# First projection whole in front of the recurrence, its input copied to DRAM in eight transfers a half; plain order in place of a permuted one in the block inverse

## The chip, the core and the metric

One NeuronCore of one Trainium2 chip runs the whole program. The metric is device time in microseconds (us), from runs of the whole program; the profile is of one more execution. Engines are named as the profile names them: PE (TensorE matmuls), PEld (its weight loads), DVE (VectorE), ACT (ScalarE), POOL (GpSimd) and SP, whose queue issues all DMA transfers.

## What is computed

A decoder trunk with one RWKV-7 layer and one differential attention layer, 1024 tokens of width 1024, all in float32. The part that the change touches is the first layer:

```
xm   = xn + (x_prev - xn) * mu[p]                      # a mix for each of p = r, k, v, g
r, k, v, g = xm[p] @ w_in[p]                           # four projections, 1024 x 1024 each
w, a = two small two-step projections of mixed inputs  # decay and rate
for t in tokens:                                       # 16 heads, state 64 x 64
    sa    = state @ a_t
    state = state * w_t + sa b_t^T + v_t k_t^T
    y_t   = state @ r_t
x = x + (groupnorm(y) + bonus) * silu(g) @ w_out
```

The second layer (shared keys and values, attention in 8 heads, output projection, final norm) follows and is not touched.

## The kernel before

**Front.** `start` loads x in eight tiles, scales and transposes it into `xnT` in SBUF. `lora` makes the two small projections (`d_c`, `d_a` in DRAM). `projections(hf, src, order, prs)` makes the large ones: for a half of the tokens `hf`, for each `p` in `order` and each block `pr` of 128 output columns, one *step* of 24 matmuls of 128x512 (three for each of 8 blocks of the contraction, since every operand is split into a high and a low part; L197, L198, L199). The first step of each group of one `p` also makes the mixed input `xm` and its two parts: two instructions on ACT (L149, L153) and two on DVE (L144, L156) for each of the 8 blocks. The string `ORD` sets how these three generators are interleaved (`s`, `l`, `f`), and where `xnT` is copied to DRAM (`0`, `1`: one transfer of 2052 KB for each half, L772), from where later steps load their input (`xk`, L756). Before the change the front holds p = 0, 2, 1 of the first half of the tokens for the column blocks 0 to 3 (`lower`).

**Recurrence.** The tokens are cut in chunks of 64. One unit of work (`Ms[n]`, 16 of them) is two chunks for 8 of the 16 heads. Each goes through `prep` (decay products `ar`, `bk`; the matrices within a chunk `pm`; the strictly triangular 32x32 blocks `ab`, by DRAM `dA` into `al` with all 128 blocks side by side), `invert` (31 steps of a triangular solve, each two instructions on POOL, L559 and L561; the result goes by DRAM `dX` into `qd`), `merge` (from 32x32 to 64x64), `chain` (the state passes through both chunks) and `norm`. `slot` emits one slot for each unit: chain of unit i, merge of i+1, invert of i+2, prep of i+3, and between them *fill* from one list: the remaining projection steps (before: the upper column blocks of the first half, then all of the second half, then the gate p = 3) and the first output projection, as much as `FILL` says for the slot. In `chain`, `out` accumulates y from two matmuls for each of 4 head pairs x 2 heads: one against the state (`sv`, 64x64, L637) and one against the solved part (`uv`, 128x64, L640).

**Permutation.** In `prep` the rows of `ar` are written permuted within blocks of 32 (`mixed`, two instructions, L476), `ab` is added through a permuted view (L518) and the mask is built for that order, so that `invert` writes a partition of `xx` to `dX` as one run of 1 KB.

**What sets the order.** A list scheduler places the instructions of each engine and the DMA issues of SP, by its own durations and by the priorities in `PRI`; each engine then runs its list in order. So an edit of `ORD` or `FILL` also changes rows far from it. All transfers are issued by SP, in one list.

Of the kernel before, what the change touches and what calls it, by code (L numbers as in the profile page):

```python
# [20 lines left out]
P = 128  # L21
# [12 lines left out]
XB = 8  # L34
ORD = "sslflsfls01llllflflflflflflflflflflfl"
FILL = [26000] * 8 + [12500] * 12
PRI = {"chain": 2000, "merge": 1500, "invert": 1000, "prep": 500}
# [27 lines left out]
def rsqrt(nc, pool, x, shape, name, steps=3, tiles=None):  # L65
# [8 lines left out]
    return y  # L74


def mixed(x):

    return x.rearrange("p c (k q) -> p c q k", q=4)


class Trunk:
# [144 lines left out]

    def projections(self, hf, src, order, prs=range(KT)):
        for p in order:
            group = {}  # L230
            for pr in prs:
                yield self.proj_step(hf, p, pr, src, group)
# [167 lines left out]
    def wkv_open(self):  # L400
# [18 lines left out]
        for r0 in (0, 64):  # L419
            v = self.pmask[r0:r0 + 64].rearrange("p a (z t) -> p a z t", z=2)  # L420
            for z, order in enumerate(([[32, 2], [1, 4], [4, 8]], [[1, 64]])):
                nc.gpsimd.affine_select(out=v[:, 0, z, :], in_=v[:, 0, z, :], compare_op=ALU.is_ge, fill=0.0,
                                        base=z - 1, channel_multiplier=-1, pattern=order)
        self.bones = cst.tile([P, P], F32, name="bones")
# [23 lines left out]
    def prep(self, M, following):  # L448
# [6 lines left out]
        def ch(x):  # L455
            return x.rearrange("p u (c t) -> p (u c) t", t=C)
# [17 lines left out]
        M["ar"] = ar = ua.tile([P, 8, 2, C], F32, name="ar")  # L474
        for b in range(0, C, 32):
            nc.vector.tensor_tensor(ar[:, :, 0, b:b + 32].rearrange("p c (q k) -> p c q k", q=4), mixed(ch(kraw)[:, :, b:b + 32]),  # L476
                                    mixed(ep[:, :, b:b + 32]), op=ALU.mult)
        nc.vector.tensor_tensor(ar[:, :, 1, :], ch(r), ep[:, :, 1:CW], op=ALU.mult)
# [36 lines left out]
        for b in range(4):  # L515
            bs = slice(32 * b, 32 * b + 32)
            av = ab[bs].rearrange("p c (k q) -> p c k q", q=4)
            nc.vector.tensor_tensor(av, av, pm[bs, b // 2, :, b % 2 * 32:b % 2 * 32 + 32].rearrange("p c (q k) -> p c k q", q=4), op=ALU.add)  # L518
        nc.sync.dma_start(out=dA.rearrange("c x s t -> (x s) c t"), in_=ab)
# [20 lines left out]
    def invert(self, M):  # L540
# [14 lines left out]
        for s in range(31):  # L555
# [6 lines left out]
            yield 0  # L562
        dX = self.dr.tile([32, 4, 8, 32], F32, name="dX")
        nc.sync.dma_start(out=dX.rearrange("x q k t -> q x (k t)"), in_=xx)
        M["qd"] = qd = self.ub.tile([P, 8, 32], F32, name="qd", bufs=1)
        nc.sync.dma_start(out=qd, in_=dX.rearrange("(c x) q k t -> (x q k) c t", c=8))

# [50 lines left out]
    def chain(self, M):  # L618
# [9 lines left out]
        def out(c):  # L628
            if c == 0:
                M["y"] = ps.tile([P, 8, C], F32, name="y", bufs=1)  # L630
            y = M["y"]
            for u in range(NU):
                uc = u * NC + c

                z = M["qt"] + c == 0
                for h in range(0 if z else 2):
                    nc.tensor.matmul(y[HS[h], uc, :], lhsT=sv[HS[h], h, uc, :], rhs=ar[HS[h], uc, 1, :], start=True, stop=False,  # L637
                                     tile_position=(h * 64, h * 64))
                for h in range(2):
                    nc.tensor.matmul(y[HS[h], uc, :], lhsT=uv[:, h, uc, :], rhs=pm[:, h, uc, 64:P], start=z, stop=True,  # L640
                                     tile_position=(0, h * 64))
        for c in range(NC):
# [95 lines left out]
    def layer1(self):  # L738
# [14 lines left out]
        def src_of(hf):  # L753
# [4 lines left out]
            return src  # L758
        lower, upper = range(KT // 2), range(KT // 2, KT)
        with ExitStack() as s1:  # L760
            xnp = s1.enter_context(tc.tile_pool(name="xnp", bufs=1, reuse_waits="tile"))
            lp = s1.enter_context(tc.tile_pool(name="lp", bufs=2, reuse_waits="tile"))
            self.fps = s1.enter_context(tc.tile_pool(name="fps0", bufs=8, space=PSUM, reuse_waits="tile"))
            xnT = xnp.tile([P, KT, S + 1], F32, name="xnT")
            start = self.start(lp, xnT)
            lo = self.lora(lp, xnT)
            first = self.run(self.projections(0, lambda k: xnT[:, k, 0:TH + 1], (0, 2, 1), lower))
            plan = {"s": start, "l": lo, "f": first}
            for c in ORD:
                if c in "01":  # L770
                    hf = int(c)
                    nc.sync.dma_start(out=d_xn[hf].rearrange("k p t -> p k t"), in_=xnT[:, :, hf * TH:hf * TH + TH + 1])  # L772
                    continue
                for _ in range(KT if c == "f" else 1):
                    next(plan[c], None)
            for g in plan.values():
                assert next(g, None) is None
# [3 lines left out]
        def steps():  # L781
            yield from self.projections(0, src_of(0), (0, 2, 1), upper)
            yield from self.projections(1, src_of(1), (0, 2, 1))
# [564 lines left out]
```

## Time and profile before

| | us |
|---|---|
| median of 3 runs | 1670.84 (1669.64 to 1671.71) |
| the profiled execution's own time | 1675.29 |
| its span, first to last instruction | 1673.6 |
| PE, DVE, ACT, POOL busy | 1538.7, 1251.5, 938.2, 691.1 |
| granted TensorE clock, mean over the span | 0.942 |

The span is the time that the views below divide up; the profiled execution has 1.7 us around it, and is 4.5 us above the median. A busy share is an average over stages with different limits; the stages are the front, a stretch in which the first preps and inverts run but no chain yet, the recurrence with its chain, and the second layer. A granted clock of 1.0 is 2.4 GHz and 0.5 is 1.2 GHz; a mean between them is a mix of the two.

### The profile page before, as it was taken

Reading aid. Unit: us, or ns where it says so; the run is one execution under the profiler, and the core shown is the slowest. Engines: PE = TensorE matmul, PEld = TensorE weight load, DVE = VectorE, ACT = ScalarE, POOL = GpSimd, SP = SyncE. Lnnn points to the kernel's source line nnn. Section 1 sums busy time; section 2 is a strip of 40 time slices with the busy share of each in tenths; the row PEclk is TensorE's granted clock in tenths of the full one; section 3 lists DMA queues with packets and bytes.
Section 4 is the critical chain, followed back from the end, with each engine's and each line's share of the span. In section 5 each row is a group of like instructions: output and inputs, shape, how many; then the busy total and the mean of one; then the engine's idle time right before and its main releaser. Section 6 shows DMA issues by size and latency. Waiting matters only on the chain.

```text
span 1673.6 us, 31316 instructions
## 1 busy us (share of the span) xinstructions
PE 1538.7 (92%) x10496; PEld 1227.3 (73%) x10496; DVE 1251.5 (75%) x3183; ACT 938.2 (56%) x2145; POOL 691.1 (41%) x1685
## 2 busy tenths in 40 slices
PE   4699978899899999999899988999999999999897
PEld 3477656677677766677698877788888888888786
DVE  7657888668785686887866767878878788777763
ACT  5556855647555566566543545665656656566421
POOL 4010116778766473787776011233332333323100
PEclk7899978999989978999899899999999999999999
DMA  7655875655565545566556652211111111103331
GB/s 190 177 190 170 247 188 165 191 146 179 167 195 159 145 134 142 171 185 188 146 166 190 178 161 89 76 45 33 45 38 32 45 33 45 39 32 114 98 123 51
DMA packets 207216, 213.70 MB, mean 128 GB/s; under 512 B 62032, under 2 KB 149328, under 8 KB 207056
## 3 DMA queue, kind: packets, MB, share of 16 engines
q1 hardware_dynamic: 207056, 211.71, 43.5%
q8 instruction: 83, 1.36, 0.3%
q14 instruction: 77, 0.63, 0.1%
HBM read 153.39 MB, written 58.27 MB: 126 GB/s over the span
## 4 chain that ended last, share of the span: by engine, by line
PE 59%; DVE 13%; DMA 11%; ACT 7%; issue 5%; POOL 4%; SPq 1%; ACTq 0%; DVEq 0%; POOLq 0%
PE pj L887 6%; PE pj L888 6%; PE pj L889 6%; PE tr L992 4%; PE fl L198 3%; PE fl L197 3%; PE fl L199 3%; PE sc L950 2%; PE sc L951 2%; PE tr L980 2%; POOL xx L561 2%; PE sc L505 2%; DMA wf<-in_a_w_in 2%; POOL tm L559 2%; PE fl L290 1%
## 5 line engine op out<-in xcount | busy, mean ns | idle before, releaser
L197 PE MATMUL fl<-xh,wh 128*128 128x512 f32 x512 | 217.3, 434 | 16.4 <-ACT xh L153 9.3
L559 POOL TENSOR_TENSOR tm<-al,xx 128x60 f32<-128x60 f32 (+24 forms) x496 | 198.7, 401 | 63.7 <-DVE xx L553 27.4
L198 PE MATMUL fl<-xl,wh 128*128 128x512 f32 x512 | 218.4, 428 | 6.2 <-DVE xl L156 6.1
L561 POOL TENSOR_TENSOR xx<-xx,tm 128x60 f32<-128x60 f32 (+24 forms) x496 | 201.9, 407 | 37.4 <-DVE xx L553 1.2
L887 PE MATMUL pj<-wh,xh 128*128 128x512 f32 x512 | 213.3, 417 | 1.6 <-ACT xh L1225 1.6
L199 PE MATMUL fl<-xh,wl 128*128 128x512 f32 x512 | 212.9, 417 | 0.1
L888 PE MATMUL pj<-wh,xl 128*128 128x512 f32 x512 | 202.3, 395 | 2.1 <-DVE xl L1226 2.1
L889 PE MATMUL pj<-wl,xh 128*128 128x512 f32 x512 | 202.0, 394 | 0.0
L956 ACT ACTIVATE p<-sc,mx 128x256 f32<-128x256 f32 (+7 forms) x128 | 94.7, 742 | 140.8 <-DVE mx L955 122.1
L162 DVE TENSOR_TENSOR wl<-wf,wh 128x512 fp32r<-128x512 f32 x160 | 116.8, 734 | 68.6 <-ACT wh L161 61.0
L936 POOL CAST kh<-kh 64x128 fp32r<-64x128 f32 x128 | 44.5, 347 | 260.8 <-ACT kh L928 256.8
L161 ACT CAST wh<-wf 128x512 fp32r<-128x512 f32 x160 | 97.8, 617 | 81.6 <-PE fl L198 51.2
L197 PEld LDWEIGHTS fl<-xh,wh 128*128 128x128 f32 x512 | 101.2, 199 | 47.8 <-ACT xh L153 11.9
L198 PEld LDWEIGHTS fl<-xl,wh 128*128 128x128 f32 x512 | 101.7, 199 | 37.3 <-DVE xl L156 10.0
L199 PEld LDWEIGHTS fl<-xh,wl 128*128 128x128 f32 x512 | 102.1, 199 | 25.1 <-issue 1.9
L889 PEld LDWEIGHTS pj<-wl,xh 128*128 128x128 f32 x512 | 96.5, 188 | 21.6
L888 PEld LDWEIGHTS pj<-wh,xl 128*128 128x128 f32 x512 | 97.0, 189 | 18.6 <-DVE xl L1226 3.3
L887 PEld LDWEIGHTS pj<-wh,xh 128*128 128x128 f32 x512 | 96.9, 189 | 17.5 <-ACT xh L1225 2.5
L954 DVE TENSOR_REDUCE mx<-sc 128x1 f32<-128x256 f32 (+7 forms) x128 | 95.6, 755 | 0.8
L992 PEld LDWEIGHTS tr<-v,p 128*128 128x128 f32 x576 | 74.9, 194 | 7.1 <-ACT p L982 2.4
L505 PE MATMUL sc<-ar,bk 64*128 64x128 f32 x512 | 64.5, 312 | 13.8 <-DVE v L532 3.7
L992 PE MATMUL tr<-v,p 128*128 128x128 f32 x576 | 76.0, 278 | 1.2 <-ACT p L982 1.2
(295 smaller groups left out, 3855.4 us busy)
## 6 DMA issues: line engine op xcount, KB each, us to landing
wf<-in_a_w_in SPq DMA_DIRECT2D x64, 512.0 KB
xk<-d_xn SPq DMA_DIRECT2D x64, 256.5 KB
d_in<-ev SPq DMA_DIRECT2D x64, 256.0 KB
wf<-in_b_w SPq DMA_DIRECT2D x64, 256.0 KB
al<-dA SPq DMA_DIRECT2D x16, 512.0 KB
wf<-in_a_w_out SPq DMA_DIRECT2D x16, 512.0 KB
p<-d_x SPq DMA_DIRECT2D x10, 512.0 KB
d_c<-cc SPq DMA_DIRECT2D x16, 260.0 KB
```

The costliest lines, as they stand in the source:

```text
L161: self.nc.scalar.copy(out=wh, in_=wf)
L162: self.nc.vector.tensor_tensor(wl, wf, wh.bitcast(F32), op=ALU.subtract)
L197: nc.tensor.matmul(G["ps"], lhsT=wh[:, kk, :], rhs=xh, start=(k == 0), stop=False)
L198: nc.tensor.matmul(G["ps"], lhsT=wh[:, kk, :], rhs=xl, start=False, stop=False)
L199: nc.tensor.matmul(G["ps"], lhsT=wl[:, kk, :], rhs=xh, start=False, stop=(k == KT - 1))
L505: nc.tensor.matmul(pp[h][:, i, :], lhsT=bkh(h, c), rhs=ar[h * 64:h * 64 + 64, c].rearrange("p z t -> p (z t)"), start=True, stop=True)
L559: nc.gpsimd.tensor_tensor(tv, al[:, s:s + 1, s + 1:].to_broadcast([P, n, w]), xx[:, 0:n, s:s + 1].to_broadcast([P, n, w]), op=ALU.mult)
L561: nc.gpsimd.tensor_tensor(xx[:, 0:n, s + 1:], xx[:, 0:n, s + 1:], tv, op=ALU.add)
L887: nc.tensor.matmul(pf, lhsT=self.X[i][0][:, k], rhs=wh, start=(k == 0), stop=False)
L888: nc.tensor.matmul(pf, lhsT=self.X[i][1][:, k], rhs=wh, start=False, stop=False)
L889: nc.tensor.matmul(pf, lhsT=self.X[i][0][:, k], rhs=wl, start=False, stop=(k == KT - 1))
L992: nc.tensor.matmul(po, lhsT=at[:, b, :], rhs=H["v"][:, b, :], start=(b == 0), stop=(b == i))
```

## The change

1. `ORD` and `projections`: the front now makes p = 0, 2, 1 of the first half for all 8 column blocks (24 steps in place of 12). The fill list loses these 12 steps and the second making of their three mixed inputs, with 24 loads of `xk`. `FILL` falls from 26000 to 19000 in the first eight slots.
2. The copies of `xnT` to DRAM are made block by block, eight transfers for each half in place of one.
3. The permutation goes: one instruction for `ar` in place of two, a plain add for `ab`, a plain mask; `dX` is laid out so that `invert` writes it in runs of 32 numbers (128 bytes).
4. `out` makes all state matmuls of a chunk first and then all `uv` matmuls, with one start flag for each head row.

```diff
-ORD = "sslflsfls01llllflflflflflflflflflflfl"
-FILL = [26000] * 8 + [12500] * 12
+ORD = "sslflsflsllll" + 10 * "flf1" + 12 * "f00"
+FILL = [19000] * 8 + [12500] * 12
...
-def mixed(x):
-    return x.rearrange("p c (k q) -> p c q k", q=4)
...
-    def projections(self, hf, src, order, prs=range(KT)):
+    def projections(self, hf, src, order):
         for p in order:
             group = {}
-            for pr in prs:
+            for pr in range(KT):
                 yield self.proj_step(hf, p, pr, src, group)
...
-        for b in range(0, C, 32):
-            nc.vector.tensor_tensor(ar[:, :, 0, b:b + 32].rearrange("p c (q k) -> p c q k", q=4), mixed(ch(kraw)[:, :, b:b + 32]),
-                                    mixed(ep[:, :, b:b + 32]), op=ALU.mult)
+        nc.vector.tensor_tensor(ar[:, :, 0, :], ch(kraw), ep[:, :, 0:C], op=ALU.mult)
...
-            av = ab[bs].rearrange("p c (k q) -> p c k q", q=4)
-            nc.vector.tensor_tensor(av, av, pm[bs, b // 2, :, b % 2 * 32:b % 2 * 32 + 32].rearrange("p c (q k) -> p c k q", q=4), op=ALU.add)
+            nc.vector.tensor_tensor(ab[bs], ab[bs], pm[bs, b // 2, :, b % 2 * 32:b % 2 * 32 + 32], op=ALU.add)
...
-        dX = self.dr.tile([32, 4, 8, 32], F32, name="dX")
-        nc.sync.dma_start(out=dX.rearrange("x q k t -> q x (k t)"), in_=xx)
+        dX = self.dr.tile([32, 8, 4, 32], F32, name="dX")
+        nc.sync.dma_start(out=dX.rearrange("x k q t -> q x k t"), in_=xx)
...
-            for u in range(NU):
-                uc = u * NC + c
-                z = M["qt"] + c == 0
-                for h in range(0 if z else 2):
-                    nc.tensor.matmul(y[HS[h], uc, :], lhsT=sv[HS[h], h, uc, :], rhs=ar[HS[h], uc, 1, :], start=True, stop=False,
-                                     tile_position=(h * 64, h * 64))
-                for h in range(2):
-                    nc.tensor.matmul(y[HS[h], uc, :], lhsT=uv[:, h, uc, :], rhs=pm[:, h, uc, 64:P], start=z, stop=True,
-                                     tile_position=(0, h * 64))
+            z = M["qt"] + c == 0
+            pairs = [(u * NC + c, h) for u in range(NU) for h in range(2)]
+            for uc, h in [] if z else pairs:
+                nc.tensor.matmul(y[HS[h], uc, :], lhsT=sv[HS[h], h, uc, :], rhs=ar[HS[h], uc, 1, :], start=uc == c, stop=False,
+                                 tile_position=(h * 64, h * 64))
+            for uc, h in pairs:
+                nc.tensor.matmul(y[HS[h], uc, :], lhsT=uv[:, h, uc, :], rhs=pm[:, h, uc, 64:P], start=z and uc == c,
+                                 stop=uc == pairs[-1][0], tile_position=(0, h * 64))
...
-            first = self.run(self.projections(0, lambda k: xnT[:, k, 0:TH + 1], (0, 2, 1), lower))
+            first = self.run(self.projections(0, lambda k: xnT[:, k, 0:TH + 1], (0, 2, 1)))
+            kept = [iter(range(KT)) for _ in range(2)]
...
-                    hf = int(c)
-                    nc.sync.dma_start(out=d_xn[hf].rearrange("k p t -> p k t"), in_=xnT[:, :, hf * TH:hf * TH + TH + 1])
+                    k = next(kept[int(c)], None)
+                    if k is not None:
+                        nc.sync.dma_start(out=d_xn[int(c)][k], in_=xnT[:, k, int(c) * TH:int(c) * TH + TH + 1])
...
-            yield from self.projections(0, src_of(0), (0, 2, 1), upper)
```

What this does to the order of the rows is seen at three places. First SP, at the start of the program: the copies of the first half (`d_xn_69`) stand before and after at the same place, behind the loads of x.

```order
L107 DMA xt<-in_x 128x1024 x4
L772 DMA d_xn_69<-xnT 128x8x513
L173 DMA wf<-in_a_w_in 128x1024
L756 DMA xk<-d_xn_69 128x513 x3
L173 DMA wf<-in_a_w_in 128x1024 x3
L209 DMA d_in_60<-ev 128x512
```

```order
L102 DMA xt<-in_x 128x1024 x4
L766 DMA d_xn_69<-xnT 128x513 x5
L168 DMA wf<-in_a_w_in 128x1024
L766 DMA d_xn_69<-xnT 128x513 x3
L168 DMA wf<-in_a_w_in 128x1024 x3
L204 DMA d_in_60<-ev 128x512
```

The one transfer has become eight in two bunches, with a weight load between them, and the three loads of `xk` that stood behind it are gone.

Second SP again, at the first load of `kk`, the input of the first prep that comes last (`d_in_61` is the projection p = 1, `d_in_60` is p = 0). Before:

```order
L209 DMA d_in_61<-ev 128x512 x2
L756 DMA xk<-d_xn_69 128x513
L173 DMA wf<-in_a_w_in 128x1024
L756 DMA xk<-d_xn_69 128x513 x2
L446 DMA kk<-d_in_61 128x4x128
L173 DMA wf<-in_a_w_in 128x1024
L756 DMA xk<-d_xn_69 128x513 x3
L209 DMA d_in_60<-ev 128x512
```

Of the change:

```order
L204 DMA d_in_61<-ev 128x512 x2
L168 DMA wf<-in_a_w_in 128x1024
L441 DMA kk<-d_in_61 128x4x128
L204 DMA d_in_61<-ev 128x512
L168 DMA wf<-in_a_w_in 128x1024
L441 DMA kk<-d_in_61 128x4x128
L438 DMA cc<-d_c 128x4x130
```

Before, the steps that follow the first `kk` are those of the upper column blocks of p = 0, whose input comes back from DRAM; in the change they are the upper blocks of p = 1 itself, and no `xk` stands there.

Third PE, in the chain, at the matmuls that accumulate `y` (`zu` are the other matmuls of a chain step). Before:

```order
L666 MATMUL zu<-uv,bkt 64x64 x8
L640 MATMUL y<-pm,uv 64x64 x2
L637 MATMUL y<-ar,sv 64x64 x2
L640 MATMUL y<-pm,uv 64x64 x2
L637 MATMUL y<-ar,sv 64x64 x2
L640 MATMUL y<-pm,uv 64x64 x2
L637 MATMUL y<-ar,sv 64x64 x2
L640 MATMUL y<-pm,uv 64x64 x2
```

Of the change:

```order
L639 MATMUL zu<-sv,pm 64x64 x8
L629 MATMUL y<-ar,sv 64x64 x8
L649 MATMUL zu<-zs,q 64x64 x8
L658 MATMUL zu<-uv,bkt 64x64
L632 MATMUL y<-pm,uv 64x64
L658 MATMUL zu<-uv,bkt 64x64 x7
L632 MATMUL y<-pm,uv 64x64 x7
```

The two kinds of y matmuls alternated in pairs and now stand in two blocks of eight, each beside a block of `zu`.

## Rows read from the trace of the kernel before

**Rows 1.** Busy us of each engine by stage, with granted clock and DMA:

```profile
core 0: us, PE busy (x) PEld busy (x) DVE busy (x) ACT busy (x) POOL busy (x), PEclk, DMA share, GB/s
100.00:196.50 96.50, 90.49 (x394) 68.79 (x391) 71.18 (x102) 71.86 (x129) 9.28 (x28) 1.00 0.69 212
196.50:313.00 116.50, 99.93 (x489) 73.50 (x489) 95.32 (x164) 67.30 (x135) 55.10 (x115) 0.87 0.67 189
313.00:962.00 649.00, 606.36 (x5845) 476.01 (x5843) 484.15 (x1124) 365.78 (x741) 425.44 (x984) 0.92 0.58 166
962.00:1673.60 711.60, 681.35 (x3524) 564.28 (x3524) 535.61 (x1681) 378.62 (x1053) 181.25 (x528) 0.98 0.21 65
```

**Rows 2.** The line of the first prep's matmuls: ns min/median/max, first and last start:

```profile
L505 PE MATMUL sc<-ar,bk x512: 272/272/580, 195.8 to 842.0; 64*128 64x128 f32 x171
```

**Rows 3.** The line of the chain's first matmuls, the same columns:

```profile
L647 PE MATMUL zu<-sv,pm x512: 222/222/270, 312.9 to 956.6; 128*64 128x64 f32 x171
```

**Rows 4.** POOL in three stretches, instructions of L559 alone (31 for each invert):

```profile
246.20:516.60 270.40, 87.55 (x217) 0.93 0.60 171
516.60:653.50 136.90, 21.86 (x62) 0.86 0.53 147
653.50:914.10 260.60, 89.33 (x217) 0.94 0.59 173
```

**Rows 5.** What POOL waited for from 516 to 655 us: total, times, longest:

```profile
POOL tm L559 <- DVE xx L553: 16.1, 2, 14.0
POOL xx L550 <- DMA dX<-xx: 15.1, 3, 9.2
```

**Rows 6.** DVE's groups in 196.5 to 313 us: busy, mean ns, idle before:

```profile
L144 DVE SCALAR_TENSOR_TENSOR xm<-xk,mug,xm 128x512 f32<-128x512 f32 x20 | 17.3, 874 | 0.8 <-ACT xm L149 0.8
L156 DVE TENSOR_TENSOR xl<-xm,xh 128x512 fp32r<-128x512 f32 x21 | 14.7, 708 | 1.3 <-ACT xh L153 1.1
...
L518 DVE TENSOR_TENSOR ab<-ab,pm 32x256 f32<-32x256 f32 x16 | 10.9, 684 | 0.2
...
L476 DVE TENSOR_TENSOR ar<-kraw,cc 128x256 f32<-128x256 f32 x6 | 3.5, 634 | 0.0
...
L478 DVE TENSOR_TENSOR ar<-r,cc 128x512 f32<-128x512 f32 x3 | 2.1, 688 | 2.3 <-DMA r<-d_in 2.3
```

**Rows 7.** PE's y groups in 313 to 962 us, the same columns:

```profile
L640 PE MATMUL y<-pm,uv 128*64 128x64 f32 x512 | 48.9, 248 | 0.6 <-DVE uv L659 0.5
L637 PE MATMUL y<-ar,sv 64*64 64x64 f32 x480 | 45.3, 250 | 0.0
```

**Rows 8.** PE in order of time around one y: start us, us, instruction, records:

```profile
950.46 0.69 PE L666 MATMUL zu<-uv,bkt 128*64 128x64 f32 x16
950.98 0.29 PE L640 MATMUL y<-pm,uv 128*64 128x64 f32 x4
...
952.77 0.39 PE L292 MATMUL fl<-wl,xh 128*128 128x256 f32 x1
```

**Rows 9.** PE in order of time at a block of `zu`:

```profile
932.31 0.95 PE L647 MATMUL zu<-sv,pm 128*64 128x64 f32 x16
933.19 0.39 PE L290 MATMUL fl<-wh,xh 128*128 128x256 f32 x1
```

**Rows 10.** SP's issues in order of time, late in the recurrence:

```profile
847.57 0.37 SPq L519 DMA_DIRECT2D dA<-ab  x1
...
850.37 0.56 SPq L536 DMA_DIRECT2D al<-dA  x1
...
914.09 0.57 SPq L564 DMA_DIRECT2D dX<-xx  x1
918.88 0.37 SPq L566 DMA_DIRECT2D qd<-dX  x1
```

**Rows 11.** SP's issues in order of time, in the front:

```profile
23.66 0.39 SPq L772 DMA_DIRECT2D d_xn<-xnT  x1
24.15 0.52 SPq L173 DMA_DIRECT2D wf<-in_a_w_in  x1
41.61 1.28 SPq L756 DMA_DIRECT2D xk<-d_xn  x3
```

More of the change, by code (lines that the diff above doesn't have):

```diff
@@ L420, in wkv_open @@
             v = self.pmask[r0:r0 + 64].rearrange("p a (z t) -> p a z t", z=2)
-            for z, order in enumerate(([[32, 2], [1, 4], [4, 8]], [[1, 64]])):
+            for z in range(2):
                 nc.gpsimd.affine_select(out=v[:, 0, z, :], in_=v[:, 0, z, :], compare_op=ALU.is_ge, fill=0.0,
-                                        base=z - 1, channel_multiplier=-1, pattern=order)
+                                        base=z - 1, channel_multiplier=-1, pattern=[[1, 64]])
         self.bones = cst.tile([P, P], F32, name="bones")
@@ L562, in invert @@
             yield 0
-        dX = self.dr.tile([32, 4, 8, 32], F32, name="dX")
-        nc.sync.dma_start(out=dX.rearrange("x q k t -> q x (k t)"), in_=xx)
+        dX = self.dr.tile([32, 8, 4, 32], F32, name="dX")
+        nc.sync.dma_start(out=dX.rearrange("x k q t -> q x k t"), in_=xx)
         M["qd"] = qd = self.ub.tile([P, 8, 32], F32, name="qd", bufs=1)
-        nc.sync.dma_start(out=qd, in_=dX.rearrange("(c x) q k t -> (x q k) c t", c=8))
+        nc.sync.dma_start(out=qd, in_=dX.rearrange("(c x) k q t -> (x k q) c t", c=8))
     def merge(self, M):
@@ L758, in src_of @@
             return src
-        lower, upper = range(KT // 2), range(KT // 2, KT)
         with ExitStack() as s1:
@@ L775, in layer1 @@
                     next(plan[c], None)
-            for g in plan.values():
+            for g in (*plan.values(), *kept):
                 assert next(g, None) is None
```

## Prediction

> **What bounds the kernel now.** I read the table of busy time by stage first. It has four stages after the first 100 us [rows 1]: a front that PE fills (90.5 of 96.5 us, clock 1.00), a stretch from 196.5 us, where the first prep's matmuls start [rows 2], to 313 us, where the first chain starts [rows 3], then the recurrence of 649 us to 962 us, and the second layer of 711.6 us. The last one does not use anything that the change moves, and I leave it as it is. So the question is where the first chain starts, and how long the recurrence takes.
>
> In the recurrence PE is busy 606 of 649 us at a clock of 0.92 [rows 1], and it looks like the bound. POOL is busy for only 425 us there, but its order tells more [rows 4]: the first seven inverts take 270.4 us, 38.6 each, and the last seven 260.6 us, 37.2 each; only the two between them take 136.9 us, 68.5 each. Each invert needs the one before it to leave POOL, and in 14 of 16 cases that is the pace. In the two slow ones POOL waits for DVE's copies into `xx`, which stand behind a late `al`, and for buffers [rows 5]: prep is late, since at this time PE has both its heaviest fill and a clock of 0.86. So there are two bounds side by side: POOL's pace of some 37.9 us for a unit, and PE's work, 606.4/16 = 37.9 us for a unit. At the pace of the others 16 inverts take 16 x 37.9 = 606 us; they take 667.9. The gap of 62 us is what the recurrence can give back without a faster invert.
>
> **The change part by part.** *Steps into the front.* Counted over the whole PE order, 366 projection matmuls stand ahead of the first prep's matmuls before and 576 in the change; ahead of the first chain 600 and 816, that is 216 more. The front takes 96.5/394 = 0.245 us for a matmul [rows 1], so the first chain starts 216 x 0.245 = 53 us later; by busy time alone (90.49/394 = 0.230) it would be 50. I take **+53**.
>
> *The stretch to the first chain.* DVE is busy 95.3 of its 116.5 us, PE idles 16.6 us and has a clock of 0.87 [rows 1]. The upper column blocks made their mixed inputs here a second time. In the DVE order 56 pairs of L144 and L156 stand ahead of the first chain's copies before and 42 in the change; 14 pairs at 0.874 + 0.708 us [rows 6] are 22 us of DVE. The plain `ar` takes one instruction of the size of L478 (0.688) in place of two of 0.634, 0.6 us less in each prep. The plain `ab` add works on 256 elements in a partition, L478 on 512, so the trace bounds its 0.684 us from below by 0.34: 0 to 1.4 us less in each prep. In all DVE loses some 25 of 95 us. What waits on it is PE, so the gain lies between nothing and PE's idle 16.6 us. I take half, **-8**, since the inverts that also fill this stretch do not get shorter by it.
>
> *The recurrence.* PE loses 216 x 0.230 = 50 us of fill. It also loses changes of form: in one y, 28 records in alternating pairs take 952.77 - 950.98 = 1.79 us, 0.26 for four, while 16 records of one form take 0.52 us, 0.13 for four [rows 8], or 0.88, 0.22 for four [rows 9]. The order has 180 changes between the two kinds of y before and none after. At 0.13 each that is 23 us, at 0.04 it is 7, out of the 992 records of the two kinds [rows 7]; I take 20, since the straight run in the same stretch is the nearest row. So PE needs 606 - 70 = 536 us, 33.5 for a unit, which is less than POOL's pace. Then prep has no reason to be late on the average, and the gap of 62 us should close. But the fill is not even. By the order the 16 units get, in 512-wide matmuls, 96, 80, 121, 63, 101, 58, 99, 61, 53, 7, 53, 64, 63, 18, 72 and 0 (before: 99, 93, 48, 117, 112, 109, 59, 43, 112, 112, 45, 34, 74, 75, 45, 48), so units with over 95 stay slow. I let 14 us of the gap stand: **-48**, bounds -15 (the gap above 68.5 - 37.9 for one invert closes by half) and -62.
>
> *The pace of the inverts.* POOL is busy 425 of 649 us, and much of the rest lies inside the inverts, where its other instructions wait for PE and DVE. With DVE and PE lighter I take 1 us of each invert's 37.9, **-16**; bounds 0 and -32.
>
> *The copies.* They stand at the same place in SP's order, and PE's order up to the second projection step is the same. Before, the 2052 KB copy was issued at 23.66 us and the load of `xk` behind it left only at 41.61 [rows 11], holding up the weight loads; now no load waits there. But PE works on other things then, so I take 0. The same bytes go out, and eight issues of some 0.39 us in place of one are 3 us of SP at a time when it waits.
>
> *The writes of `dX`.* They are now 1024 runs of 128 bytes in place of 128 runs of 1 KB, on the way from an invert to its merge. The trace has such a write: `dA` is 1024 runs of 128 bytes, and the load behind it is issued 850.37 - 847.57 = 2.8 us later, while behind `dX` as it is now it was 918.88 - 914.09 = 4.8 us, with nothing between [rows 10]. So the row gives **0**. The Trainium skill (DMA: Bandwidth & Descriptors, Specifications) says that below 512 bytes a transfer is a read-modify-write and loses line rate, which speaks against the change. By it each write would move twice its bytes; the row for `dA` shows no sign of this, though one late row is little.
>
> The end of the recurrence I leave alone: the last unit has no fill from the first layer now, but projection matmuls of the second layer stand in its chain instead.
>
> **Sum.** 53 - 8 - 48 - 16 = -19 us. The profiled execution took 1675.3 us, so it would take 1656.3; it lies 4.5 us above the median, and against that the sum gives 1670.8 - 19 = **1652 us**.
>
> **Rivals.** *The gap stays (slower).* The late preps are not PE's fault but that of a long list of waits in one slot, and the uneven fill makes new ones: with 121, 101 and 99 matmuls in three early units and 7, 18 and 0 in late ones, PE is short of time first and idle, at the lower clock, later. For it: the low clock in just the stretch of the slow inverts, and POOL's equal pace elsewhere, which a lighter PE does not change. Against it: the heaviest units were four with 109 or more and are now one. The front's 53 us are paid in any case. The point from which it decides: if less than 53 - 8 - 16 = 29 us of the gap closes, the kernel is slower. With 10 us closed and no faster invert it is 53 - 8 - 10 = +35, so 1706 us; its cases reach from 1674 to that.
>
> *Everything gives.* The gap closes whole, the inverts take 2 us less each, the stretch to the first chain loses 15 us: 53 - 15 - 62 - 32 = -56, 1615 us. For it: DVE's relief also holds in the recurrence. Against: POOL's own busy time and the long units.
>
> *Work only moved.* The projection matmuls cost on PE the same wherever they stand. If PE was the only bound, +53 in front and -50 behind cancel, and what the lighter DVE gives is lost on uneven fill: 1671 us within 0.2%, that is 3.3 us, about what a measurement of this kernel can tell from no change.
>
> *The small runs cost.* If `dX` moved twice its 128 KB, 128 KB more at the recurrence's 166 GB/s [rows 1] are 0.8 us a write, 13 us for 16 if each is waited for: -19 + 13 = -6, 1665 us. By the rule of the Trainium skill (DMA: Bandwidth & Descriptors, Specifications) this is what would happen; the `dA` row speaks against it.
>
> **How the numbers follow.** I give the forecast 0.50 (own range 1639 to 1666: the sum with the gap's closing 13 us less, or that much more from the pace), everything gives 0.12, the small runs 0.07, work only moved 0.09, the gap stays 0.22. Faster by over 0.2% is 0.50 + 0.12 + 0.07 = 0.69, the same 0.09, slower 0.22. The range reaches to 1626 below, half of the second rival, and to 1684 above, which takes in the nearer third of the slower cases; about 2 in 10 is left out.
>
> **What would show it.** The first chain should start near 313 + 53 - 8 = 358 us, with a front at clock 1.00 until about 250 us. The inverts should follow each other on POOL at 36 to 38 us with no pair over 60, and the last chain should end near 943 us. The y lines should lose some 20 us together, L470 stand at about 0.69 us and L510 under 0.68. The load of `qd` should be issued no later behind the `dX` write than before. I am wrong if the first chain starts after 370 us, if inverts still wait for late `al`, or if PE's idle time moves into the late units with little fill.

## The result, and the profile after

The changed kernel takes **1650.96 us** (median of 4 runs, 1647.57 to 1653.18) against 1671.28 us for the kernel before (median of 4 runs, 1669.64 to 1673.72): a ratio of **0.9877 [0.9861, 0.9894]**, so it is faster by 20.3 us. The prediction was 1652 us. Its profiled execution took 1651.33 us with a span of 1649.5 us.

First the table of busy time by stage of the changed kernel, cut at its own first prep matmul, first chain and last y; it answers to [rows 1].

```profile
core 0: us, PE busy (x) PEld busy (x) DVE busy (x) ACT busy (x) POOL busy (x), PEclk, DMA share, GB/s
100.00:241.40 141.40, 139.76 (x621) 110.51 (x618) 80.27 (x116) 82.50 (x146) 7.90 (x28) 1.00 0.60 193
241.40:336.10 94.70, 91.49 (x481) 69.14 (x480) 75.50 (x133) 60.32 (x123) 50.27 (x102) 0.93 0.74 204
336.10:943.90 607.80, 539.31 (x5682) 436.26 (x5681) 441.31 (x1105) 337.80 (x692) 398.44 (x996) 0.91 0.58 162
943.90:1649.50 705.60, 671.13 (x3470) 556.14 (x3470) 532.18 (x1653) 375.43 (x1047) 182.23 (x528) 0.98 0.20 63
```

The first prep starts 45.6 us later than before (241.4 against 195.8), the stretch to the first chain is 22 us shorter (94.7 against 312.9 - 195.8 = 117.1), the recurrence 41 us shorter (607.8 against 649.0) and the second layer 6 us shorter (705.6 against 711.6). 45.6 - 22.4 - 41.2 - 6.0 = -24.0, up to rounding the difference of the two spans; the profiled execution before lay 4.0 us above the median of the four runs, the one after 0.4 us above its own, and so the medians differ by 20.

The lines of the first prep's and the first chain's matmuls of the changed kernel (ns min/median/max, first and last start), which answer to [rows 2, 3]:

```profile
L498 PE MATMUL sc<-ar,bk x512: 271/272/580, 241.4 to 823.5; 64*128 64x128 f32 x171
L639 PE MATMUL zu<-sv,pm x512: 221/222/368, 336.1 to 932.2; 128*64 128x64 f32 x171
```

Then the inverts, in two halves of eight: the first line of their step alone (31 for each invert), as in [rows 4].

```profile
core 0: us, POOL busy (x), PEclk, DMA share, GB/s
276.00:586.30 310.30, 99.98 (x248) 0.93 0.63 177
586.30:899.80 313.50, 85.99 (x248) 0.87 0.57 158
```

The sixteen now follow each other with one pace, 38.8 and 39.2 us each. The two that took 68.5 us each are gone. From the start of the first to the end of the last they take 623.6 us, against 667.9 before; but the inverts themselves are not faster: from its first step to its last one takes 38.7 us on the average, against 37.2 before. (The *own time* of an invert below is this time, first step to last; a *gap* is what lies between the last step of one and the first of the next, 72 us in all before.) What POOL does in that time is seen in two pairs of views. Busy time from the first invert's start to the last one's end, before and after:

```profile
246.20:914.10 667.90, 622.10 (x5647) 481.74 (x5646) 499.09 (x1073) 376.04 (x753) 472.22 (x1088) 0.92 0.58 167
```

```profile
276.10:899.70 623.60, 556.14 (x5549) 444.77 (x5548) 456.12 (x1038) 350.25 (x714) 442.13 (x1091) 0.90 0.60 167
```

And what POOL waited for in the same times (total, times, longest); first two lines of before, then the largest of after, which answer to [rows 5]. The first line of before is from the whole time; the second is from the slow stretch, 516 to 655 us, where it stands between the two lines of [rows 5] and is as long as they are; the prediction did not read it:

```profile
POOL xx L550 <- DMA dX<-xx: 39.2, 10, 9.2
```

```profile
POOL m L485 <- ACT m L469: 15.7, 2, 14.7
```

```profile
POOL xx L542 <- DMA dX<-xx: 51.5, 12, 10.4
POOL st L666 <- DVE tn L661: 15.5, 8, 5.3
POOL m L478 <- ACT m L464: 13.9, 5, 4.3
POOL bk L486 <- PE sc L518: 11.8, 4, 5.1
...
POOL tm L551 <- DVE xx L545: 4.7, 1, 4.7
```

POOL's busy time (the last pair of numbers before the clock) falls by 30 us, from 472.2 to 442.1. Of the waits that made the gap, that for DVE's copies into `xx` is now 4.7 us, and that for ACT's `m`, another input made in prep, 13.9 us with none over 4.3. What remains as the largest wait is the memset of a new `xx`, which must let the write of `dX` from the same buffer finish. Of its 39.2 us before, 15.1 lay in the slow stretch [rows 5], which leaves 24 inside the other inverts; now it is 51.5 us.

The y groups on PE in the recurrence, the answer to [rows 7] (busy, mean ns, idle before):

```profile
L632 PE MATMUL y<-pm,uv 128*64 128x64 f32 x512 | 32.3, 237 | 0.0
L629 PE MATMUL y<-ar,sv 64*64 64x64 f32 x480 | 25.2, 230 | 0.2 <-ACT yt L675 0.2
```

DVE's groups in the stretch from 241.4 to 336.1 us, the answer to [rows 6]:

```profile
L139 DVE SCALAR_TENSOR_TENSOR xm<-xk,mug,xm 128x512 f32<-128x512 f32 x14 | 10.9, 785 | 2.7 <-ACT xm L144 2.7
...
L151 DVE TENSOR_TENSOR xl<-xm,xh 128x512 fp32r<-128x512 f32 x13 | 10.2, 796 | 0.1
L510 DVE TENSOR_TENSOR ab<-ab,pm 32x256 f32<-32x256 f32 x16 | 6.8, 426 | 0.2
...
L470 DVE TENSOR_TENSOR ar<-kraw,cc 128x512 f32<-128x512 f32 x2 | 1.4, 680 | 0.0
```

And SP's issues of the last `dX` write and the `qd` load behind it, the answer to the last two of [rows 10]:

```profile
899.75 0.57 SPq L556 DMA_DIRECT2D dX<-xx  x1
...
904.59 0.38 SPq L558 DMA_DIRECT2D qd<-dX  x1
```

The distance is 4.8 us, as it was behind this last write; over all sixteen writes it differs, as u_perm shows below.

### The profile page after: what moved, and what is told of

The parts are those of the page before. It is cut to its first block, busy times and chain, and to the rows that moved or that the text cites. A ratio compares the mean times of both kernels' runs of the same rounds, so it can differ in the third digit from the quotient of the medians.

```text
span 1649.5 us, 31097 instructions
## 1 busy us (share of the span) xinstructions
PE 1502.5 (91%) x10496; PEld 1217.7 (74%) x10496; DVE 1194.1 (72%) x3119; ACT 910.2 (55%) x2095; POOL 658.9 (40%) x1685
## 4 chain that ended last, share of the span: by engine, by line
PE 60%; DVE 13%; DMA 10%; POOL 6%; ACT 5%; issue 5%; SPq 1%; POOLq 0%; DVEq 0%; ACTq 0%
PE pj L881 6%; PE pj L880 6%; PE pj L882 6%; PE fl L192 5%; PE fl L193 5%; PE fl L194 5%; PE tr L985 4%; POOL xx L553 3%; POOL tm L551 2%; DMA dX<-xx 2%; PE sc L943 2%; PE sc L944 2%; PE tr L973 2%; DMA xm<-d_o 2%; PE sc L498 1%
## 5 line engine op out<-in xcount | busy, mean ns | idle before, releaser
L192 PE MATMUL fl<-xh,wh 128*128 128x512 f32 x512 | 211.8, 419 | 10.6 <-DVE ev L217 8.9
L193 PE MATMUL fl<-xl,wh 128*128 128x512 f32 x512 | 212.5, 416 | 3.1 <-DVE xl L151 2.9
L551 POOL TENSOR_TENSOR tm<-al,xx 128x60 f32<-128x60 f32 (+24 forms) x496 | 186.0, 375 | 43.6 <-DVE xx L545 4.7
L553 POOL TENSOR_TENSOR xx<-xx,tm 128x60 f32<-128x60 f32 (+24 forms) x496 | 187.9, 379 | 37.2 <-DVE xx L545 1.1
L943 PE MATMUL sc<-kh,q 128*128 128x512 f32 (+2 forms) x192 | 71.0, 378 | 1.8 <-DVE q L927 1.3
```

Of the source, the lines that this page charges most:

```text
L192: nc.tensor.matmul(G["ps"], lhsT=wh[:, kk, :], rhs=xh, start=(k == 0), stop=False)
L193: nc.tensor.matmul(G["ps"], lhsT=wh[:, kk, :], rhs=xl, start=False, stop=False)
L551: nc.gpsimd.tensor_tensor(tv, al[:, s:s + 1, s + 1:].to_broadcast([P, n, w]), xx[:, 0:n, s:s + 1].to_broadcast([P, n, w]), op=ALU.mult)
L553: nc.gpsimd.tensor_tensor(xx[:, 0:n, s + 1:], xx[:, 0:n, s + 1:], tv, op=ALU.add)
L943: nc.tensor.matmul(sc[:, b:e], lhsT=q[:, m], rhs=H["kh"][:, m, b:e], start=True, stop=False)
```

## The experiments

Two theories stood against each other. **Theory 1:** POOL's row of inverts is the bound of the recurrence; the new front gains because prep is no longer late for it, and PE's own time in the recurrence matters little now. **Theory 2:** PE's time (or a transfer) is the bound, and the gain comes from the y order and the lighter PE. Every ratio below is to the kernel before, run on the same chip, and stands beside the 0.9877 [0.9861, 0.9894] of the change. The change itself was repeated on one of the three chips only, that of c_again, c_wt and a_fill2. A repetition of the change gave nearly the same:

**The change again (a_again).** No edit. 

> The changed kernel itself once more, on the chip of the next three kernels. It should stand at 0.986 to 0.990 of before again; what the others are worth is read against this run.

Measured: 1649.55 us, ratio 0.9874 [0.983, 0.9918]. The inverts' own times add to 618.7 us (619.4 in the first profile), the first chain starts at 330.8 us (336.1). So a start may move by 5 us from one execution to the next, and the plan behind it is stable.

**The old front (u_front).**

```diff
-ORD = "sslflsflsllll" + 10 * "flf1" + 12 * "f00"
-FILL = [19000] * 8 + [12500] * 12
+ORD = "sslflsfls01llllflflflflflflflflflflfl"
+FILL = [26000] * 8 + [12500] * 12
...
+            first = self.run(self.projections(0, lambda k: xnT[:, k, 0:TH + 1], (0, 2, 1), lower))
...
+            yield from self.projections(0, src_of(0), (0, 2, 1), upper)
```

The copies are whole again, too; the plain order and the y order stay. 

> The changed kernel with the old front: column blocks 0 to 3 alone, the two whole copies, FILL at 26000; the plain order and the y blocks stay. Theory 1 (POOL's pace): the first chain starts some 40 us earlier than in the change, the stretch before it is again near 110 us, and two or three inverts again wait for a late al, 30 to 60 us in all; in sum 5 to 20 us slower than the change. Theory 2 (PE's work): the same work on PE, so within 4 us of the change.

Measured: 1671.82 us, ratio 0.9967 [0.9941, 0.9993]. Its stages, and its inverts (the first line of their step):

```profile
191.90:307.40 115.50, 101.26 (x489) 73.73 (x488) 92.20 (x162) 68.20 (x137) 53.51 (x113) 0.87 0.67 194
307.40:947.70 640.30, 588.01 (x5847) 473.54 (x5847) 466.75 (x1111) 371.35 (x746) 409.93 (x986) 0.90 0.60 167
947.70:1661.40 713.70, 682.29 (x3523) 564.46 (x3523) 536.38 (x1682) 379.06 (x1053) 182.23 (x528) 0.98 0.21 65
```

```profile
239.50:533.55 294.05, 97.25 (x248) 0.93 0.61 175
533.55:626.20 92.65, 12.42 (x31) 0.89 0.57 160
626.20:897.10 270.90, 82.12 (x217) 0.90 0.61 165
```

What follows: with the old front the stretch to the first chain is as long as before (115.5 us, DVE busy 92.2 of them), the second layer too (713.7), and a gap of 41 us is back around one invert, the ninth. The first chain starts 29 us earlier than in the change, not 40 as expected. So the front, with its copies and its `FILL`, makes 0.9 of the 1.2 per cent, and the shorter stretch and more than half of the closed gap come with it. The other two parts together are worth 0.33 per cent, between 0.07 and 0.59. The profiled execution is the fastest of the ten, 8.6 us below their median, so that its trace shows less of the loss than the ratio.

**The alternating y back (u_y).**

```diff
-            for uc, h in [] if z else pairs:
-                nc.tensor.matmul(y[HS[h], uc, :], lhsT=sv[...], ..., start=uc == c, stop=False, ...)
-            for uc, h in pairs:
-                nc.tensor.matmul(y[HS[h], uc, :], lhsT=uv[...], ...)
+            for u in range(NU):
+                uc = u * NC + c
+                for h in range(0 if z else 2):
+                    nc.tensor.matmul(y[HS[h], uc, :], lhsT=sv[...], ..., start=True, stop=False, ...)
+                for h in range(2):
+                    nc.tensor.matmul(y[HS[h], uc, :], lhsT=uv[...], ..., start=z, stop=True, ...)
```

> The changed kernel with the y matmuls alternating in pairs again, as before. Theory 1 (POOL sets the pace: in the changed kernel the inverts follow each other on POOL without gaps, so that PE has time to spare): PE gets some 20 us of work back, the inverts still run back to back at 38 to 39 us, and the time rises by 0 to 6 us. Theory 2 (PE's work sets the pace): the time rises by the 20 us.

Measured: 1660.43 us, ratio 0.9881 [0.9835, 0.9928]. The stage of the recurrence, and its y groups:

```profile
333.80:953.60 619.80, 567.57 (x5685) 446.43 (x5684) 444.32 (x1105) 341.38 (x696) 411.91 (x1004) 0.90 0.57 159
```

```profile
L633 PE MATMUL y<-pm,uv 128*64 128x64 f32 x512 | 51.0, 255 | 0.0
L630 PE MATMUL y<-ar,sv 64*64 64x64 f32 x480 | 46.2, 257 | 0.4 <-ACT sv L617 0.3
```

PE is busy 28 us more in the recurrence, and the ratio is 0.0004 above that of the change, where 28 us would be 0.017; the interval leaves room for some 9 us. So PE's time is hidden for the most part: this speaks for theory 1. What came through in the profile is one gap of 11.5 us between two inverts.

**The permutation back (u_perm).** The two `ar` instructions, the permuted `ab` add and mask, and `dX` in runs of 1 KB.

```diff
-        dX = self.dr.tile([32, 8, 4, 32], F32, name="dX")
-        nc.sync.dma_start(out=dX.rearrange("x k q t -> q x k t"), in_=xx)
+        dX = self.dr.tile([32, 4, 8, 32], F32, name="dX")
+        nc.sync.dma_start(out=dX.rearrange("x q k t -> q x (k t)"), in_=xx)
```

> The changed kernel with the permutation back (two instructions for ar, the permuted add for ab, writes of dX in runs of 1 KB). Theory 1 (POOL's pace): DVE gets some 30 us back over 16 preps; the stretch before the first chain gets 3 to 6 us longer and the inverts keep their pace, so 3 to 8 us slower. Theory 2 (PE's work): no change, since PE does the same. Theory 3 (the writes of 128 bytes are dear): the wait between the write of dX and the load of qd falls by 1 us or more and the kernel gets up to 13 us faster.

Measured: 1653.06 us, ratio 0.9831 [0.9779, 0.9884]: within the uncertainty the same as the change, and so not the 3 to 8 us slower of theory 1. SP's issues of the last `dX` write and its load, then the wait of POOL's memset and the busy time over all inverts:

```profile
904.54 0.57 SPq L564 DMA_DIRECT2D dX<-xx  x1
...
908.37 0.38 SPq L566 DMA_DIRECT2D qd<-dX  x1
```

```profile
POOL xx L550 <- DMA dX<-xx: 36.3, 9, 9.4
```

```profile
276.40:902.30 625.90, 568.96 (x5651) 455.94 (x5650) 480.15 (x1062) 353.14 (x720) 466.77 (x1091) 0.90 0.60 168
```

The last load leaves 3.8 us behind its write, in place of 4.8. One pair is not enough to go by, since the kernel before writes the same runs of 1 KB and has 4.8 there [rows 10]. Over all sixteen pairs the shortest distance is 3.5 us here and 3.4 in the kernel before, and 4.7 in the change; ten of the sixteen are under 4.7 here, three in the kernel before and none in the change. So runs of 1 KB can let the load go some 1 us sooner, but often the order of the other issues hides it. POOL waits 15 us less for these writes, but the inverts are no faster (625.9 against 623.6 us): POOL is busy 25 us more and DVE 24 us more. The Trainium skill (DMA: Bandwidth & Descriptors, Specifications) says that below 512 bytes a transfer is a read-modify-write; the traces agree in the direction, 4.7 against 3.5 us at the shortest, and show no cost of it in the time.

**One copy for each half (u_copies, then c_again, the same kernel).**

```diff
-                    if k is not None:
-                        nc.sync.dma_start(out=d_xn[int(c)][k], in_=xnT[:, k, ...])
+                    if k == KT - 1:
+                        nc.sync.dma_start(out=d_xn[hf].rearrange("k p t -> p k t"), in_=xnT[:, :, ...])
```

> The changed kernel with one transfer of 2052 KB for each half in place of eight, at the place where the last of the eight stood in the program. Theory 1: the copies are hidden behind PE's first stage, 0 within 3 us. Rival: the pieces let the first weights land earlier, and without them PE waits in the first 100 us, 5 us or more slower.

> The kernel with two whole copies once more. In its first profile the first 241 us were as in the change (first prep at 241.3 and 241.4 us) and the 7 us came later, in the recurrence. Theory: the copies cost nothing in themselves, and the planner made another order of the recurrence; then the two kernels differ by under 8 us here, and again not in the first 241 us. Rival: eight transfers cost 16 us, as the ratios of the first runs say.

Measured: 1640.49 us, ratio 0.9779 [0.9742, 0.9815], and in the repetition 1644.0 us, 0.9837 [0.9785, 0.9889], where the change on the same chip took 1649.55 us. First prep (241.3 and 244.2 us) and first chain (333.7 and 338 us) stand where they were. So the eight small copies do not help, and neither expectation of u_copies had whole ones faster. The whole ones took 5.5 us less than the change on the same chip: within the uncertainty of the two ratios, but all four runs (1641.4 to 1647.3) lie below all four of the change (1648.0 to 1654.1). The 16 us of the first ratio were not confirmed. What differs is the plan of the recurrence: its inverts add to 613.6 and 615.9 us, with no gap. That the copies themselves cost nothing is in line with that, not shown.

**More work on POOL (a_more).** The memset of `xx` is made nine times, 8 x 0.316 us x 16 = 40 us more; the added work changes nothing in the output.

```diff
-        nc.gpsimd.memset(xx, 0.0)
+        for _ in range(9):
+            nc.gpsimd.memset(xx, 0.0)
```

> The changed kernel with the memset of xx on POOL done nine times instead of once: 8 x 0.315 us more for POOL in each of 16 inverts, 40 us in all, the result the same. Theory 1 (POOL's inverts set the pace): 25 to 40 us slower, since POOL is busy for only 41% of the span but has no slack in the recurrence. Theory 2 (PE's work, or the chain's own waits, set the pace): 0 to 5 us slower.

Measured: 1678.54 us, ratio 1.0023 [1.0002, 1.0044], which is 0.0146 or 24 us above the change. All inverts, as in the view of after:

```profile
274.70:931.40 656.70, 575.30 (x5617) 458.54 (x5616) 464.80 (x1044) 355.10 (x723) 470.35 (x1201) 0.88 0.58 160
```

The inverts take 33 us longer and stand back to back. Theory 2 would have it nearly hidden, since POOL is busy only 470 of 657 us. The 24 us are just below what theory 1 put as the least, and of 40 us of work 16 stayed hidden.

**Less work on POOL (a_wt).** One multiplication of the state update (`st`, 30 instructions of 0.74 us) moves from POOL to DVE.

```diff
-                nc.gpsimd.tensor_tensor(wt, tn, wb, op=ALU.mult)
+                nc.vector.tensor_tensor(wt, tn, wb, op=ALU.mult)
```

> The changed kernel with the state update wt = tn * wb on DVE instead of POOL. POOL loses 30 instructions of 0.74 us in the recurrence, 22 us, and 17 us of waiting for tn. Theory 1: the inverts take 1 to 2 us less each and the kernel gets 15 to 35 us faster. Theory 2: DVE gets 20 us more on the chain's way, 0 to 10 us slower.

Measured: 1637.78 us, ratio 0.978 [0.9733, 0.9827], by the ratios 16 us below the change, and with the first run of whole copies (0.9779) the lowest here. The profiled execution, 1629.76 us, is the fastest of its four. All inverts, and POOL's largest waits in the recurrence:

```profile
273.20:877.60 604.40, 548.06 (x5526) 437.75 (x5525) 463.40 (x1060) 349.57 (x715) 426.14 (x1062) 0.91 0.62 172
```

```profile
POOL xx L542 <- DMA dX<-xx: 41.6, 8, 9.7
POOL bk L486 <- PE sc L518: 24.8, 6, 14.1
```

The inverts take 19 us less, their own times add to 566.0 us (619.4 in the change), but 38 us of gaps between them have come up: prep is late again (POOL's longest wait for PE's `sc`, a matmul of prep, is 14.1 us). POOL and prep are both near the bound.

**Both at once (c_wt).** Whole copies and the state update on DVE.

> Two whole copies, and the state update on DVE. If POOL's queue sets the pace, this adds up: 20 to 35 us faster than the change, 1616 to 1632 us where before is 1671. If PE's order is the bound by now, no faster than the state update on DVE alone (0.978 of before).

Measured: 1646.65 us, ratio 0.9847 [0.9802, 0.9892]. The two gains do not add: on the same chip whole copies alone took 1644.0 us, so that here the state update on DVE gained nothing. The inverts' own times add to 563.3 us, but with gaps of 6.4, 11.9, 7.7 and 10.3 us, then 54 us (44 in the change) from the last invert to the last y, and a second layer of 713 us. The inverts have outrun their preps: POOL waited 22.2 us for DVE's copies into `xx`, 4.7 in the change.

**The memset on DVE (a_msd).**

```diff
-        nc.gpsimd.memset(xx, 0.0)
+        nc.vector.memset(xx, 0.0)
```

> The changed kernel with the memset of xx on DVE instead of POOL. On POOL this memset waits in the middle of the next invert for the write of dX to land, 50.9 us in 11 waits. Theory 1: these leave POOL's pace, 20 to 50 us faster. Theory 2: no change. Rival to theory 1: DVE waits in POOL's place, and what stands behind it on DVE is late; then 0 to 20 us slower.

Measured: 1655.96 us, ratio 0.9884 [0.9836, 0.9932]: no gain. POOL's 51.5 us of waits for `dX` are gone, and the inverts' own times add to 622.3 us all the same. POOL's waits in the recurrence, then DVE's largest:

```profile
POOL st L666 <- DVE tn L661: 28.5, 16, 6.1
...
POOL bk L486 <- PE sc L518: 23.4, 6, 6.2
```

```profile
DVE xx L542 <- DMA dX<-xx: 26.2, 6, 7.6
```

The wait has moved to DVE, and POOL's other instructions wait for DVE and PE in its place.

**The planner told that the `dX` write takes longer (a_plan).** Its own duration for it rises by 4 us, so that the memset is placed later.

```diff
-            back = any(f"name='{n}" in str(i.ins[0]) for n in ("dA", "dX"))
+            back = any(f"name='{n}" in str(i.ins[0]) for n in ("dA", "dX")) or "name='dX" in str(i.outs[0])
```

> The changed kernel with the planner told that the write of dX takes 4 us longer (as its reads already do); the program does the same work. Theory 1: the planner puts the memset of xx later into the next invert, POOL's waits of 50.9 us shrink, 10 to 40 us faster. Theory 2: no change within 4 us.

Measured: 1652.95 us, ratio 0.9867 [0.9827, 0.9908]: no clear change. No wait of the memset is left among POOL's, the inverts' own times add to 606.8 us, 12.6 less; 8.3 us of gaps (3.2 in the change) and 6.8 us more in the stretch to the first chain take most of it back.

**Another place of the fill (a_fill2).**

```diff
-FILL = [19000] * 8 + [12500] * 12
+FILL = [22000] * 8 + [10500] * 12
```

> The changed kernel with the fill moved forward: FILL 22000 in the first eight slots and 10500 in the last twelve, 302000 in all as in the change. Theory 1: in the first units PE needs more than POOL's 38 us, gaps between inverts come back, and late units run short of fill; 5 to 15 us slower. Rival: where the budget puts the fill matters little, since the planner orders it anew; within 4 us.

Measured: 1665.87 us, ratio 0.9961 [0.9939, 0.9983], 16 us above the change on the same chip. Its inverts:

```profile
276.90:588.30 311.40, 97.19 (x248) 0.93 0.65 175
588.30:680.10 91.80, 22.10 (x62) 0.96 0.64 181
680.10:915.00 234.90, 65.09 (x186) 0.82 0.53 145
```

The same steps in the front, and the same work of PE, but more of the fill early: behind the eighth invert gaps of 14.5, 3.8 and 4.7 us open, and behind them PE is at a mean clock of 0.82. The sum of `FILL` is the same, so where `FILL` puts the fill counts by itself; how much of the front's gain hangs on it is not shown.

## Why the prediction was right, and where its terms were off

The mechanism was right in its first half. The front's steps were paid in front, and the gap between the slow inverts closed, because prep was no longer late (u_front brings 41 us of gap back, a_fill2 23 us). The inverts then follow each other on POOL, and POOL's row is nearer to the bound than PE: 28 us more of PE cost some 9 us at most (u_y), 40 us more of POOL cost 24 (a_more). That less work on POOL helps is not as well shown: 22 us less gained 16 (a_wt), but nothing when it was done beside whole copies (c_wt). And the row is not POOL's own work alone: inside the inverts of the change POOL idles 177 of 619 us, and of the chain of work that ended last the profile's page puts 6% of the span on POOL (4% before) and 60% on PE, with DVE at 13% and DMA at 10%. The sum of -19 met -20 of the medians, but by terms that were off in both directions; that the number came out so near is luck:

- *Steps into the front, +53.* Measured +45.6. The matmuls of the longer front cost 141.4/621 = 0.228 us each, nearer the price by busy time (0.230) that was put aside; in the longer front PE idles 1.6 us of 141. The term was worked out with the 216 matmuls more ahead of the first chain, while 45.6 us is how far the first prep moved; by the order 210 matmuls more stand ahead of that, and 210 x 0.228 = 48.
- *The stretch to the first chain, -8, bounds 0 and -16.6.* Measured -22, beyond the bound. DVE's relief came near the estimate (95.3 to 75.5 us, 20 where 25 were put), but the terms behind it were not those given: the 14 pairs were counted over the whole time ahead of the first chain, and in this stretch the two lines of the mixed inputs lost 11 us, not 22; `ab`'s add lost 4, within its bounds, and work of other lines that had stood there made up the rest. What failed is "the gain lies between nothing and PE's idle 16.6 us": PE's idle time fell from 16.6 to 3.2 us, as it could by that rule, but its busy time fell too, from 99.9 to 91.5, in step with its clock (0.87 to 0.93). The bound left the clock out.
- *The gap, -48, bounds -15 and -62.* It closed whole: of 72 us between inverts before (10 of them POOL's own work) 3 are left. The fear for heavy units did not come true in the change itself; a_fill2 shows that it was near. (By the prediction's own list five units, not four, had 109 matmuls or more before.)
- *The pace of the inverts, -16, bounds 0 and -32.* Wrong in sign: the inverts' own times add to 619.4 us, 595.2 before. The step was "with DVE and PE lighter I take 1 us of each invert's 37.9". The lighter DVE did help: POOL's step instructions took 26.7 us less, 1.7 us for each invert, for the reason given under what was not expected. POOL's busy time fell by 30 us in all; with the 10 us that stood in the gaps left out, inside the inverts from 462 to 442. But its idle time inside them rose from 595 - 462 = 133 to 619 - 442 = 177 us, and 27 of these 44 are the memset's wait for the last `dX` write (24 to 51). There are two buffers for `xx`, so the memset for the next invert must wait for the write of the one before the invert that runs; with no gap between inverts that write has only just left. That this wait is the price by itself is not so: a_msd takes it from POOL and gains nothing, a_plan takes it and gains 12.6 us in the inverts, not in the time. Which wait would have to go for a shorter invert stays open; a third buffer for `xx`, which would tell, wasn't tried.
- *The y order, 20 of PE's 70 us.* PE's load in the recurrence fell to 539 us, where 536 were put. The two y lines lost 37 us together (94.2 to 57.5), not 20, and by u_y the order is worth 28 us of PE. By the order's 180 changes of kind that is an estimated 0.16 us for each, near the 0.13 of [rows 8]. The Trainium skill (TensorEngine Tiling (Array Packing), Key Properties) says that a change of tiling mode drains TensorE; the traces agree that changes cost PE time, 28 us here. The sum did not price it by itself, rightly: most of it is hidden.
- *The copies, 0,* and *the writes of `dX`, 0.* The change has no cost from the writes that the time shows, though at the shortest the load leaves 4.7 us behind the write, and 3.5 with runs of 1 KB (u_perm). The row for `dA`, 2.8 us, was too low for either. The rival of the small runs is not needed. The copies' 0 holds within the uncertainty of the ratios; if they have a price, it is a loss of some 5 us.
- *The second layer, left alone.* It gave 6 us. Its first projection matmuls (`pj`) stand in the last chain, as the fence below shows; the prediction saw them there and did not price them. With 54 matmuls fewer in the layer PE is busy 10 us less there (681.4 to 671.1). With the old front the layer is long again (u_front, 713.7 us), but in c_wt, with the new front, it is 713 us too, with PE busy for 680.5: so it seems to hang on how many of its matmuls the planner puts into the last chain, not on the front as such.

PE in order of time at the end of the changed kernel's last chain:

```profile
942.88 0.40 PE L881 MATMUL pj<-wh,xl 128*128 128x512 f32 x1
943.20 0.68 PE L632 MATMUL y<-pm,uv 128*64 128x64 f32 x14
943.81 0.50 PE L882 MATMUL pj<-wl,xh 128*128 128x512 f32 x1
```

Of what was to be seen: the front at clock 1.00 to 241 us (put at 250), the last chain's end at 943.9 (943), no pair of inverts over 60 us and the last `qd` load no later behind its write came as put; the first chain came at 336, not 358, and the inverts at 39 us, not 36 to 38. L510 fell to 0.43 us; L470 stands at 0.68. The two misses, some 22 us each way, cancelled: the recurrence was to give 64 us and gave 41.

## What to carry to other kernels

Where one engine runs a long serial job for each unit and the others prepare it, look for pairs of units that are far apart: the gap between them is what a lighter preparation can give back, and the pace of the others is what it cannot. Then ask what stood in the gap: work and waits of the same queue that were free there can move into the job when it closes. A bound for a stretch from "idle time of the engine that waits" holds only at a fixed clock.

## What was not expected of the hardware

- Behind a write of 128 KB from 128 partitions to DRAM in runs of 128 bytes the load went 4.7 us after the write at the soonest, behind one in runs of 1 KB 3.5 us (change and u_perm, issue to issue, sixteen writes each).
- POOL's step instructions, the same 992 of the same shapes, take 187.9 + 186.0 us in the change, 201.9 + 198.7 before, 201.0 + 198.8 in u_perm and 198.5 + 192.0 in u_copies, which has the plain order as well. So the permutation alone does not set it. What does can be read from the traces: whether DVE works at the same time. Two steps of one shape in the change, and the DVE instruction beside the second:

```profile
447.06 0.34 POOL L553 TENSOR_TENSOR xx<-xx,tm 128x66 f32<-128x66 f32 x1
464.88 0.64 POOL L553 TENSOR_TENSOR xx<-xx,tm 128x66 f32<-128x66 f32 x1
```

```profile
464.56 0.79 DVE L157 TENSOR_TENSOR wl<-wf,wh 128x512 fp32r<-128x512 f32 x1
```

In the change 252 of the 992 steps meet no DVE instruction at all and take on the average 3 ns more than the shortest of their shape; 339 meet one of DVE's large instructions with two inputs in SBUF (`wl`, `xl`, `xm`, `ar`, `bk`, `a`, `al`, `ab`) and take in the median 331 ns more. The shortest times of all 992 add to 274 us in the change and in the kernel before; what lies above that is 100 us in the change, 93 of it in the 339 steps, and 126 us before, 117 of it in 387 steps. So this is where the lighter DVE of the change made POOL faster. In u_copies, with the plain order, 367 steps meet such an instruction, and 106 us lie there: how often the two meet also hangs on the plan.
- Taking a wait from POOL's in-order queue did not take its time from the kernel: of 51.5 us taken in a_msd nothing came out, while of 40 us added in a_more 24 did.
